# Sample rows of the input projection as fp32 products on four column strips, and one add ahead of the sums of squares

## The chip, the core and the metric

The kernel runs on one core of one Trainium2 chip. The metric is device time in microseconds, the median of repeated runs; the profile is of one further execution, and all rows below come from it. The engines are TensorE (PE, with its weight loads PEld), VectorE (DVE), ScalarE (ACT), GpSimd (POOL) and SyncE (SP, which issues most of the loads).

## What is computed

One step of a decoder layer with width 1024 on 2048 prompt rows and 32 sample rows (8 sequences of 4 tokens). Both sets of rows go through the same input projection, whose 3072 columns are six blocks of 512, and then through their own attention and retention:

```python
hp = rms_norm(xp, norm_mix_g[l], NORM_EPS)
dq, dk, dv, rq, rk, rv, rg = project_mixer_inputs(hp, w_in[l], *tab_p)
...
hs = rms_norm(xs, norm_mix_g[l], NORM_EPS)
sq, sk, sv, tq, tk, tv, tg = project_mixer_inputs(hs, w_in[l], *tab_s)
```

with

```python
y = xf * lax.rsqrt(jnp.mean(xf * xf, axis=-1, keepdims=True) + eps)
...
z = h @ w_in_l
dq, dk, dv, rq, rk, rv, rg = jnp.split(z, SPLIT_POINTS, axis=-1)
```

All tensors are fp32. The per-row factor of the norm is applied after the product, to its result; only the gain g is multiplied into the rows before it.

## The kernel before

The program is: projection, mixer (attention and retention, decode of the sample rows, output projection), and the two halves of the FFN. `projection` runs over four token groups g of 512 rows (four tiles of 128), and in each over the six blocks of 512 weight columns in the order 1, 2, 0, 3, 4, 5 (keys, values, queries, retention q and k, retention v, gate). "First block", "fourth block" and so on below count in that order.

Precision: every fp32 operand of a large product is split into a high part in the type fp32r and the rest (`split`, L121 to L124: a cast on ACT, a subtraction on DVE), and a product is three fp32r products, h.wh, l.wh and h.wl (`terms`, L292, lines L296 to L298). A block has 1024 rows of weights, loaded as four panels kp of two 128-row slices (512 KB each) into the tile `wr` of pool `early`, which has two buffers (`load_w`, L174; the load is L176 on SP), and split into `wh` and `wl` with six buffers each. A tile of tokens takes 24 products of 512 columns (8 slices k, 3 terms) into one bank of PSUM with the tag `z`, of which there are four. In the first block of a group the four tiles go side by side (k is the outer loop), so all four banks are in use; in the others one tile after the other.

The 32 sample rows are a fifth tile (t = NQ) in group 0 only. Their columns of x are loaded (`xsr`, L206), squared (`xsq`, L208), multiplied by the gain and split into `xs`, with the high and low halves side by side as 64 columns; `sample_terms` (L307 to L309) multiplies these 64 columns with `wh` and with `wl`, 16 products a block, into a fifth `z` bank. `fold` (L300) copies the first 32 partitions of the result and adds the second 32 (`add_halves`). This tile is the last of each block in group 0.

The factor of the norm: the squares of x are added up over the panels in `sq` [128, 2, 512] (L195, L197). `scales` (L217) multiplies each of its eight 128-column pieces with a column of ones (L221, eight plain fp32 products of one column, two accumulating per tile), the same for the sample rows (L226), copies the sums and takes the power -0.5 on POOL (`rsqrt_mean`). The results `rstd` and `rstd8` are what the first reader of `z` scales with: `krow` in `put_qk` (L318) on ACT for queries and keys.

Retention per prompt tile (`retention`, L379) runs in the fifth block and uses two banks with the tag `r`. The FFN has two products for the sample rows that are already in the form of plain fp32 on strips: L1207, tile `sz`, four strips of 32 rows, 256 columns, two rounds; and L1314, tile `sacc`, strips of 32 rows, 512 columns.

Most of the order on each engine is set by a scheduler when the kernel is built: it takes the program's order and the dependences and places each instruction by its own estimate of times, and each engine then runs its list strictly in that order. `keep_in_program_order` pins single instructions. A buffer of a tile tag goes to the next tile when the last reader is done.

## Time and profile before

| | |
|---|---|
| time, median of 3 runs | 2707.18 us (2699.53 to 2709.26) |
| profiled execution, its own time | 2718.03 us |
| its span | 2716.3 us |
| mean granted clock of PE | 0.984 of full speed |
| busy PE / DVE / ACT / POOL | 2617.5 / 1526.0 / 1064.9 / 1009.1 us |
| chain that ended last: PE / DVE / DMA / ACT | 85% / 4% / 4% / 3% |
| projection, fp32r products of the prompt rows (L296 to L298) | 768 of each of three lines, about 303 us a line |
| projection, products of the sample rows (L308, L309) | 48 of each line |

How to read it: a plain fp32 product of the program shows as two records in the trace, an fp32r product as one. A record's duration contains the filling of the array, so the time that a product holds PE is read from start to start of neighbours: 0.23 us for 512 columns at full clock, where each record is 0.39 us long. The stages lie at 0 to about 680 us (projection), to 1360 (mixer), to 2270 (first half of the FFN) and to the end. In the timelines the number in front is the start from the span's begin, the second the length; a bracket gives the idle time of the engine before the row and what ended it. An SP row is the issue of a transfer, not its length.

### The profile page before, as it was taken

The numbers are of one execution on the slowest core, as the hardware profiler recorded it, in microseconds if no ns is written. First come the engines' busy times: TensorE is split into PE (matmuls) and PEld (weight loads), VectorE is DVE, ScalarE is ACT, GpSimd is POOL, SyncE is SP. The second block draws the span as 40 slices with busy tenths as digits, with TensorE's granted clock in tenths as the row PEclk, the third lists the DMA queues.
The fourth block names the chain that finished last, engine by engine and source line by source line (L and its number), as shares of the span: only waits on it lengthen the run. The fifth ranks groups of instructions, "written<-read, shape, count | busy, mean of one in ns | idle before, by whom it ended". The sixth has DMA issues, their size and how long they took to land.

```text
span 2716.3 us, 35504 instructions
## 1 busy us (share of the span) xinstructions
PE 2617.5 (96%) x13180; PEld 2097.4 (77%) x13180; DVE 1526.0 (56%) x2296; ACT 1064.9 (39%) x2051; POOL 1009.1 (37%) x1032
## 2 busy tenths in 40 slices
PE   8999999999888999997989999999999999999998
PEld 6777788787666888886768778786777777788886
DVE  5554544543667677675365555585665665345364
ACT  4343343432556555554243233352332333333342
POOL 1000000011662133324456556557877884003111
PEclk9999999999899999999999999999999999999999
DMA  7436545364995464624442222354434436744463
GB/s 240 129 105 186 155 146 152 113 182 128 257 254 132 129 170 126 156 81 155 133 182 83 96 101 86 105 174 171 148 131 167 149 130 216 257 143 148 141 208 120
DMA packets 166347, 413.35 MB, mean 152 GB/s; under 512 B 19376, under 2 KB 54896, under 8 KB 164384
## 3 DMA queue, kind: packets, MB, share of 16 engines
q1 hardware_dynamic: 100176, 259.63, 29.3%
q0 software_dynamic: 56784, 147.27, 18.6%
q10 hardware_dynamic: 9216, 4.20, 0.6%
q8 instruction: 104, 1.70, 0.3%
q14 instruction: 67, 0.55, 0.1%
HBM read 287.95 MB, written 123.08 MB: 151 GB/s over the span
## 4 chain that ended last, share of the span: by engine, by line
PE 85%; DVE 4%; DMA 4%; ACT 3%; issue 3%; POOL 2%; ACTq 0%; SPq 0%; POOLq 0%; DVEq 0%
PE fps L1162 27%; PE ops L1378 15%; PE z L298 7%; PE z L297 7%; PE z L296 7%; PE op L854 4%; PE sp L796 2%; PE sp L799 2%; PE atp L843 2%; PE cz L956 2%; PE cz L955 2%; PE cz L957 1%; ACT p L814 1%; DMA w<-w_ffn_out 1%; PE op L399 1%
## 5 line engine op out<-in xcount | busy, mean ns | idle before, releaser
L1162 PE MATMUL fps<-xh,wh 128*128 128x512 f32 x1232 | 485.2, 396 | 4.5 <-ACT xh L123 4.5
L1162 PE MATMUL fps<-xh,wl 128*128 128x512 f32 x1232 | 482.2, 391 | 0.0
L1162 PE MATMUL fps<-xl,wh 128*128 128x512 f32 x1232 | 481.4, 391 | 0.0
L296 PE MATMUL z<-wh,xh 128*128 128x512 f32 x768 | 302.9, 396 | 8.5 <-ACT xh L190 8.5
L298 PE MATMUL z<-wl,xh 128*128 128x512 f32 x768 | 303.6, 396 | 0.0
L297 PE MATMUL z<-wh,xl 128*128 128x512 f32 x768 | 302.6, 394 | 0.0
L1162 PEld LDWEIGHTS fps<-xh,wh 128*128 128x128 f32 x1232 | 232.2, 189 | 71.1 <-issue 11.6
L1162 PEld LDWEIGHTS fps<-xh,wl 128*128 128x128 f32 x1232 | 232.0, 188 | 58.3 <-issue 9.2
L1162 PEld LDWEIGHTS fps<-xl,wh 128*128 128x128 f32 x1232 | 232.2, 188 | 47.1
L124 DVE TENSOR_TENSOR xl<-xl,xh 128x1024 fp32r<-128x1024 f32 (+1 forms) x133 | 149.3, 1145 | 203.7 <-ACT xh L123 203.7
L1378 PE MATMUL ops<-vh,xh 128*128 128x512 f32 x616 | 239.6, 392 | 6.8 <-ACT u L1406 4.7
L1378 PE MATMUL ops<-vh,xl 128*128 128x512 f32 x616 | 239.7, 391 | 0.0
L1378 PE MATMUL ops<-vl,xh 128*128 128x512 f32 x616 | 238.3, 391 | 0.0
L124 DVE TENSOR_TENSOR wl<-w,wh 128x512 fp32r<-128x512 f32 x132 | 150.4, 1150 | 119.0 <-ACT wh L123 118.9
L800 DVE TENSOR_REDUCE mx<-sp 128x1 f32<-128x1024 f32 (+4 forms) x192 | 168.7, 908 | 83.9 <-PE sp L799 66.1
L124 DVE TENSOR_TENSOR wl<-wt,wh 128x512 fp32r<-128x512 f32 x176 | 194.7, 1111 | 30.4 <-ACT wh L123 30.4
L123 ACT CAST xh<-xl 128x1024 fp32r<-128x1024 f32 (+1 forms) x133 | 111.6, 868 | 221.5 <-DMA xl<-hop_d 200.2
L123 ACT CAST wh<-wt 128x512 fp32r<-128x512 f32 x176 | 109.1, 621 | 193.2 <-PE fps L1162 163.6
L124 DVE TENSOR_TENSOR wl<-wr,wh 128x1024 fp32r<-128x1024 f32 x96 | 117.2, 1222 | 109.4 <-ACT wh L123 107.7
L296 PEld LDWEIGHTS z<-wh,xh 128*128 128x128 f32 x768 | 144.7, 189 | 38.7 <-ACT xh L190 8.5
L123 ACT CAST wh<-w 128x512 fp32r<-128x512 f32 x132 | 81.8, 620 | 229.3 <-PE fps L1162 185.7
L298 PEld LDWEIGHTS z<-wl,xh 128*128 128x128 f32 x768 | 144.8, 188 | 31.7 <-issue 0.7
(308 smaller groups left out, 5008.7 us busy)
## 6 DMA issues: line engine op xcount, KB each, us to landing
wr<-w_in SPq DMA_DIRECT2D x96, 512.0 KB
w<-w_ffn_in SPq DMA_DIRECT2D x44, 1024.0 KB
xl<-hop_d SPq DMA_DIRECT2D x77, 512.0 KB
hop_d<-so POOLq DMA_DIRECT2D x88, 256.0 KB
kst<-k_d POOLq DMA_DIRECT2D x36, 512.0 KB
hop_d<-h POOLq DMA_DIRECT2D x66, 256.0 KB
qd<-q_d POOLq DMA_DIRECT2D x64, 256.0 KB
xop_d<-xt POOLq DMA_DIRECT2D x56, 256.0 KB
```

Of the source, the lines that this page charges most:

```text
L123: nc.scalar.copy(hi, src)
L124: nc.vector.tensor_tensor(lo, src, hi.bitcast(F32), ALU.subtract)
L296: mm(z, h[:, j, c], wh[:, j], start=k == 0, stop=False)
L297: mm(z, l[:, j, c], wh[:, j], start=False, stop=False)
L298: mm(z, h[:, j, c], wl[:, j], start=False, stop=k == KT - 1)
L796: nc.tensor.matmul(sp[:, o : o + nn], q[:, 2 * mp, sl], k, start=True, stop=False)
L799: nc.tensor.matmul(sp[:, o : o + nn], q[:, 2 * mp + 1, sl], k, start=False, stop=True)
L800: nc.vector.tensor_reduce(mx[:, c : c + 1], sp[:, :w], AX.X, ALU.max, negate=True)
L843: nc.tensor.transpose(tp[:, j, :], pt[b // 8][0][:, P * (b % 8) : P * (b % 8) + P], self.ident)
L854: self.nc.tensor.matmul(st["o"], ats[(b - lo) // 4][:, (b - lo) % 4, :], vs[b // 4][:, b % 4, :], start=b == 0, stop=b == st["i"],)
L1162: i = nc.tensor.matmul(bank, w[:, c], v, start=first and k == 0 and n == 0, stop=k == half - 1 and n == 2, skip_group_check=True,)
L1378: nc.tensor.matmul(bank, x[:, c], w, start=first and n == 0, stop=end and n == 2, skip_group_check=True)
```

## The change

- The sample rows of a block are now eight plain fp32 products of the unsplit rows (`xsr`, gain multiplied in, 32 columns) with the unsplit weight panels (`samples`). Slice k = 4 half + q goes to strip q, that is to partitions 32 q to 32 q + 31 of one bank; each strip adds up two slices. The bank has the tag `r` instead of `z`. `samples(b)` is called at the head of a block instead of in the place of the fifth tile; in each half the strips are written 3, 2, 1, 0, and 2, 1 and 0 are pinned in that order.
- `fold` adds up four strips instead of two halves: one copy and three adds.
- `xs` and its split are gone.
- In group 0 the panels kp 2 and 3 have buffers of their own (`wr2`, two), so that four raw panels are there at once. In the other groups all four panels use the two buffers `wr` as before. In group 0 a panel's buffer is now also held until the sample products have read it.
- In `scales` the two halves of `sq` are added on DVE first; four products of one column take the place of eight.

```diff
--- before.py
+++ after.py
@@ -171,8 +171,17 @@
                 self.rope_t = {4 * g + i: rp[:, i] for i in range(4)}
                 self.rope_t[NQ] = rope_s
 
+                raws = {}
+                if g == 0:
+                    sa = tc.tile_pool(reuse_waits="tile", name="sa", bufs=1)
+                    sap = sa.__enter__()
+
                 def load_w(b, kp):
-                    wr = early.tile([P, 2, 512], F32, tag="wr", name="wr", bufs=2)
+                    if g == 0 and kp > 1:
+                        wr = sap.tile([P, 2, 512], F32, tag="wr2", name="wr2", bufs=2)
+                    else:
+                        wr = early.tile([P, 2, 512], F32, tag="wr", name="wr", bufs=2)
+                    raws[b, kp] = wr
                     nc.sync.dma_start(wr, a["w_in"][b, :, 2 * kp : 2 * kp + 2, :])
                     wh = pw.tile([P, 2, 512], F32R, tag="wh", name="wh", bufs=6)
                     wl = pw.tile([P, 2, 512], F32R, tag="wl", name="wl", bufs=6)
@@ -200,15 +209,28 @@
                     if kp == 0:
                         nc.gpsimd.dma_start(rp, a["rope"][:, 4 * g : 4 * g + 4])
                 if g == 0:
-                    sa = tc.tile_pool(reuse_waits="tile", name="sa", bufs=1)
-                    sap = sa.__enter__()
                     xsr = sap.tile([P, KT, NS], F32, name="xsr")
                     nc.sync.dma_start(xsr, a["xt"][:, :, S:])
                     xsq = sap.tile([P, KT, NS], F32, name="xsq")
                     nc.scalar.activation(xsq, xsr, AF.Square)
-                    xs = sap.tile([P, KT, 2, NS], F32R, name="xs")
                     nc.vector.tensor_tensor(xsr, xsr, bc(gmix, 2, [P, KT, NS]), ALU.mult)
-                    self.split(xs[:, :, 0], xs[:, :, 1], xsr)
+
+                def samples(b):
+                    z = ps.tile([P, 512], F32, tag="r", name="zsm", bufs=2)
+                    for half in range(2):
+                        for q in (3, 2, 1, 0):
+                            k = 4 * half + q
+                            i = nc.tensor.matmul(
+                                z[NS * q : NS * q + NS],
+                                xsr[:, k, :],
+                                raws[b, k // 2][:, k % 2],
+                                start=half == 0,
+                                stop=half == 1,
+                            )
+                            if q < 3:
+                                keep(i)
+                    return z
+
                 ss = rows.tile([P, 8], F32, tag="ss", name="ss", bufs=2)
                 rstd = rows.tile([P, 8], F32, tag="rstd", name="rstd", bufs=2)
                 rstd8 = rows.tile([P, 8], F32, tag="rstd8", name="rstd8", bufs=2)
@@ -216,11 +238,9 @@
 
                 def scales():
                     sp = ps.tile([P, 8], F32, tag="tp", name="ssp", bufs=2)
+                    nc.vector.tensor_tensor(sq[:, 0], sq[:, 0], sq[:, 1], ALU.add)
                     for i in range(4):
-                        for j in range(2):
-                            nc.tensor.matmul(
-                                sp[:, i : i + 1], sq[:, j, P * i : P * i + P], ones, start=j == 0, stop=j == 1
-                            )
+                        nc.tensor.matmul(sp[:, i : i + 1], sq[:, 0, P * i : P * i + P], ones, start=True, stop=True)
                     if g == 0:
                         for k in range(KT):
                             nc.tensor.matmul(sp[:NS, 4:5], xsq[:, k], ones, start=k == 0, stop=k == KT - 1)
@@ -239,6 +259,8 @@
                     if bi:
                         for kp in range(KT // 2):
                             load_w(b, kp)
+                    if g == 0:
+                        zsm = samples(b)
                     first = []
                     if bi == 0:
                         first = [ps.tile([P, 512], F32, tag="z", name="z", bufs=4) for _ in range(4)]
@@ -251,17 +273,12 @@
                         m = NS if t == NQ else P
                         if i < len(first):
                             z = first[i]
+                        elif t == NQ:
+                            z = self.fold(rows, zsm, 512)
                         else:
                             z = ps.tile([P, 512], F32, tag="z", name="z", bufs=4)
                             for k in range(KT):
-                                if t < NQ:
-                                    self.terms(z, xh, xl, wts, b, k, i)
-                                    continue
-                                wh, wl = wts[b, k // 2]
-                                both = xs[:, k].rearrange("p c q -> p (c q)")
-                                self.sample_terms(z, both, wh[:, k % 2], wl[:, k % 2], k == 0, k == KT - 1)
-                        if t == NQ:
-                            z = self.fold(rows, z, 512)
+                                self.terms(z, xh, xl, wts, b, k, i)
                         r1 = rstd[:m, i : i + 1]
                         r8 = rstd8[:m, i : i + 1]
                         if b in (0, 1):
@@ -301,7 +318,8 @@
         nc = self.nc
         zs = pool.tile([NS, n], F32, tag="zs", name="zs", bufs=1)
         nc.vector.tensor_copy(zs, z[:NS, :n])
-        self.add_halves(zs, z, 1)
+        for q in range(1, 4):
+            nc.vector.tensor_tensor(zs, z[NS * q : NS * q + NS, :n], zs, ALU.add)
         return zs
 
     def sample_terms(self, z, both, wh, wl, first, last):
```

The scheduler moves instructions as well. Three places follow, each of the list before and of the list now; the lists are those of the program, without times, and a number behind a name tells buffers apart.

PE at the end of token group 0. Before, the last sample product (`xs` with the last `wl`) and the first products of group 1 behind it:

```order
L309 MATMUL z_1610<-wl_1447,xs_318 64x512
L296 MATMUL z_1701<-wh_1644,xh_1636 128x512 [waits Activation_49]
L297 MATMUL z_1701<-wh_1644,xl_1637 128x512
L298 MATMUL z_1701<-wl_1645,xh_1636 128x512
L296 MATMUL z_1702<-wh_1644,xh_1636 128x512 [waits Activation_49]
L297 MATMUL z_1702<-wh_1644,xl_1637 128x512
L298 MATMUL z_1702<-wl_1645,xh_1636 128x512
```

Now: the last retention tile's `up`, the sixth group of sample products (`zsm`, reading the raw panels `wr` and `wr2`), and the first product of group 1:

```order
L428 MATMUL up_1373<-rv_1343,kd_1371 64x128 [waits DVE_49]
L428 MATMUL up_1373<-rv_1343,kd_1371 64x128 x3
L223 MATMUL zsm_1414<-wr_1396,xsr_314 32x512 [waits DMAHW2_49,DVE_49]
L223 MATMUL zsm_1414<-wr_1396,xsr_314 32x512
L223 MATMUL zsm_1414<-wr_1390,xsr_314 32x512 [waits DMAHW1_49]
L223 MATMUL zsm_1414<-wr_1390,xsr_314 32x512
L223 MATMUL zsm_1414<-wr2_1408,xsr_314 32x512 [waits DMAHW4_49]
L223 MATMUL zsm_1414<-wr2_1408,xsr_314 32x512
L223 MATMUL zsm_1414<-wr2_1402,xsr_314 32x512 [waits DMAHW3_49]
L223 MATMUL zsm_1414<-wr2_1402,xsr_314 32x512
L313 MATMUL z_1659<-wh_1602,xh_1594 128x512 [waits Activation_49]
```

The first product of group 1 waited for ACT's `xh` and `wh` in both. The sample products of the sixth block stand behind all 576 prompt products of group 0, and the first of them waits for DVE to have read the `r` bank of the last retention tile. Those of the other five blocks stand in one piece at the head of their block (in the first after 47 products), except that in the fourth four transposes stand between the first four and the last four.

SP at the same place. Before: the four weight loads of group 1's first block, with an `xr` load between them, and the stores `cat_d` of the gated retention rows of group 0 behind them:

```order
L176 DMA wr_1642<-w_in 128x1024 [waits DMAHW3_49,DVE_49]
L176 DMA wr_1658<-w_in 128x1024 [waits DMAHW4_49,DVE_49]
L185 DMA xr_1666<-xt 128x2x512 [waits Activation_49]
L176 DMA wr_1674<-w_in 128x1024 [waits DMAHW5_49,DVE_49]
L176 DMA wr_1690<-w_in 128x1024 [waits DMAHW6_49,DVE_49]
L377 DMA cat_d_72<-ro_1204 128x512 [waits DVE_49]
L377 DMA cat_d_72<-ro_1270 128x512 [waits DVE_49]
L377 DMA cat_d_72<-ro_1336 128x512 [waits DVE_49]
L185 DMA xr_1682<-xt 128x2x512 [waits DVE_49]
```

Now: the four loads of the sixth block of group 0, the stores, and then the first two loads of group 1, `wr_1600` and `wr_1616`:

```order
L185 DMA wr_1390<-w_in 128x1024 [waits DMAHW1_49,DMAHW6_49,DVE_49,PE_49]
L185 DMA wr_1396<-w_in 128x1024 [waits DMAHW5_49,PE_49]
L185 DMA wr2_1402<-w_in 128x1024 [waits DMAHW0_49,DVE_49,PE_49]
L185 DMA wr2_1408<-w_in 128x1024 [waits DMAHW7_49,PE_49]
L395 DMA cat_d_72<-ro_1183 128x512 [waits DVE_49]
L395 DMA cat_d_72<-ro_1249 128x512 [waits DVE_49]
L395 DMA cat_d_72<-ro_1315 128x512 [waits DVE_49]
L185 DMA wr_1600<-w_in 128x1024 [waits DMAHW2_49,PE_49,Activation_49]
L185 DMA wr_1616<-w_in 128x1024 [waits DMAHW1_49,PE_49]
```

The loads of group 1's first block moved from ahead of the stores to behind them, and wait for PE now, where they waited for DVE.

PE at the sums of squares of group 1. Before, `z_1701` to `z_1704` are the four tiles of the first block; the sums stand in the middle of their products, 61 behind the start of the block:

```order
L296 MATMUL z_1704<-wh_1676,xh_1668 128x512
L297 MATMUL z_1704<-wh_1676,xl_1669 128x512
L298 MATMUL z_1704<-wl_1677,xh_1668 128x512
L296 MATMUL z_1701<-wh_1676,xh_1668 128x512
L221 MATMUL ssp_1753<-ones_237,sq_1633 128x1 [waits DVE_49]
L221 MATMUL ssp_1753<-ones_237,sq_1633 128x1 x7
L297 MATMUL z_1701<-wh_1676,xl_1669 128x512
L298 MATMUL z_1701<-wl_1677,xh_1668 128x512
L296 MATMUL z_1702<-wh_1676,xh_1668 128x512
```

Now the four tiles are `z_1659` to `z_1662`, and `z_2017` is the first tile of the second block:

```order
L313 MATMUL z_1662<-wh_1650,xh_1642 128x512
L314 MATMUL z_1662<-wh_1650,xl_1643 128x512
L315 MATMUL z_1662<-wl_1651,xh_1642 128x512
L243 MATMUL ssp_1711<-ones_237,sq_1591 128x1 [waits DVE_49]
L243 MATMUL ssp_1711<-ones_237,sq_1591 128x1 x3
L313 MATMUL z_2017<-wh_1995,xh_1594 128x512 [waits Activation_49]
L314 MATMUL z_2017<-wh_1995,xl_1595 128x512
L315 MATMUL z_2017<-wl_1996,xh_1594 128x512
L313 MATMUL z_2017<-wh_1995,xh_1594 128x512
```

The sums moved behind all 96 products of the first block. In groups 2 and 3 they stand after 69 and 64 products (58 and 58 before), in group 0 after 84 (82).

In the mixer's first part, where the decode of the sample rows is woven into the attention, the lists hold the same instructions in another order. Behind that they agree.

## Rows read from the trace of the kernel before

**Rows 1.** The page, part 1: busy us (share) and instructions by engine

```profile
PE 2617.5 (96%) x13180; PEld 2097.4 (77%) x13180; DVE 1526.0 (56%) x2296; ACT 1064.9 (39%) x2051; POOL 1009.1 (37%) x1032
```

**Rows 2.** Waits of PE, 8 to 680 us: total us, times, longest

```profile
PE z L296 <- ACT xh L190: 8.5, 1, 8.5
PE sop L475 <- DMA sr<-state_ret: 0.7, 1, 0.7
```

**Rows 3.** Windows: us, busy of PE, PEld, DVE, ACT, POOL, PEclk, DMA share, GB/s

```profile
191.00:680.00 489.00, 488.18 (x2399) 392.12 (x2397) 231.69 (x480) 173.94 (x308) 50.12 (x67) 1.00 0.53 154
680.00:900.00 220.00, 189.72 (x1309) 140.51 (x1310) 140.13 (x284) 124.18 (x322) 102.72 (x128) 0.92 0.76 204
```

**Rows 4.** Timeline of PE, 33 to 43 us: start, us, instruction, [idle before]

```profile
35.09 0.40 PE L308 MATMUL z<-wh,xs 128*64 128x512 f32 x1
38.77 0.40 PE L296 MATMUL z<-wh,xh 128*128 128x512 f32 x1
```

**Rows 5.** Timeline of PE around one strip group of the FFN's input, 1420 us

```profile
1420.92 0.39 PE L1162 MATMUL fps<-xh,wl 128*128 128x512 f32 x1
1421.24 1.07 PE L1207 MATMUL sz<-w,xs 128*32 128x256 f32 x16
1422.24 0.50 PE L1162 MATMUL fps<-xh,wh 128*128 128x512 f32 x1
1422.58 0.40 PE L1162 MATMUL fps<-xl,wh 128*128 128x512 f32 x1
```

**Rows 6.** Timeline of PE around two strip groups of the FFN's second product

```profile
1883.74 1.93 PE L1314 MATMUL sacc<-w,hs 128*32 128x512 f32 x6 [2.74 <-DMA w<-w_ffn_out]
1885.60 0.80 PE L1162 MATMUL fps<-xh,wh 128*128 128x512 f32 x1
...
1925.85 1.06 PE L1314 MATMUL sacc<-w,hs 128*32 128x512 f32 x6
1926.84 0.50 PE L1162 MATMUL fps<-xh,wh 128*128 128x512 f32 x1
```

**Rows 7.** Timeline of PE around the sums of squares of group 0

```profile
29.42 1.84 PE L221 MATMUL ssp<-ones,sq 128*128 128x1 f32 x16
31.19 0.67 PE L226 MATMUL ssp<-ones,xsq 128*32 128x1 f32 x16
31.79 0.50 PE L297 MATMUL z<-wh,xl 128*128 128x512 f32 x1
```

**Rows 8.** Groups of DVE by form: busy us, mean ns, idle us before

```profile
L141 DVE TENSOR_TENSOR rot<-rot,rtmp 128x512 f32<-128x512 f32 x16 | 11.0, 688 | 0.2
```

**Rows 9.** Timeline of SP, issues of weight loads

```profile
190.46 0.33 SPq L176 DMA_DIRECT2D wr<-w_in  x1
194.65 0.38 SPq L176 DMA_DIRECT2D wr<-w_in  x1
```

**Rows 10.** Timeline of ACT, the casts that waited for those loads, and krow

```profile
33.63 1.27 ACT L318 ACTIVATE krow<-z,rstd 128x512 f32<-128x512 f32 x2 [6.38 <-POOL rstd L119]
...
194.09 1.05 ACT L123 CAST wh<-wr 128x1024 fp32r<-128x1024 f32 x1 [1.49 <-DMA wr<-w_in]
201.21 1.05 ACT L123 CAST wh<-wr 128x1024 fp32r<-128x1024 f32 x1 [4.31 <-DMA wr<-w_in]
```

**Rows 11.** Timeline of PE around two idle stretches

```profile
890.01 0.50 PE L796 MATMUL sp<-kst,qd 128*128 128x512 f32 x1 [2.56 <-ACT p L814]
...
1838.83 1.44 PE L1314 MATMUL sacc<-w,hs 128*32 128x512 f32 x6 [2.82 <-DMA w<-w_ffn_out]
1840.19 0.80 PE L1162 MATMUL fps<-xh,wh 128*128 128x512 f32 x1
1842.87 0.40 PE L1162 MATMUL fps<-xh,wh 128*128 128x512 f32 x1
```

**Rows 12.** Windows of the stretch 50 to 70 us, columns as above

```profile
50.00:60.00 10.00, 10.00 (x48) 8.05 (x47) 1.32 (x4) 2.23 (x4) 2.56 (x4) 1.00 1.03 263
60.00:70.00 10.00, 10.00 (x45) 7.35 (x45) 3.63 (x4) 3.35 (x4) 0.00 (x0) 1.00 0.88 268
```

## Prediction

> **What bounds the kernel now.** I read the page's busy shares first, then PE's waits, then the table by stage, then the timelines of PE, SP and ACT where the change acts. PE is busy for 96% of the span, DVE for 56% [rows 1]. In the projection that is tighter still: from 8 to 680 us PE waits twice, once for its first operand at the start and once for 0.7 us [rows 2], and from 191 to 680 us it is busy for 488.2 of 489 us at full clock [rows 3]. So in this stage time on PE is time, and anything added to DVE or ACT is free until PE has to wait for it. In the mixer's first 220 us the opposite holds: PE stands idle for 30.3 us and the clock is at 0.92 [rows 3]; the decode rows are woven in there.
>
> **Part 1, the sample products.** One block's 16 products last from 35.09 to 38.77 us, 3.68 us, right up to the next product [rows 4]; six blocks are 22.1 us. What takes their place has a model in the FFN: plain fp32 products of 32 columns on strips. Three strips of 512 columns (six records, two a product) hold PE 0.99 us at full clock and 1.86 us at half [rows 6]. The difference, 0.87 us, is what one round over the strips streams at full clock, however many strips take part. Eight products of 256 columns, two rounds on four strips, go from 1421.24 to 1422.24 us [rows 5]: 1.00 us for two half rounds, so the fourth strip is free too. The group also starts 0.09 us late against the 0.23 us step of its neighbours, and the product behind it takes 0.34 us instead of 0.23: 0.33 us of edges in all beyond the 0.87. A block of the new kind has two full rounds, 2 x 0.87 + 0.33 = 2.07 us, six 12.4, and 0.3 more because the group of the fourth block is cut by four transposes in the order. Gain: 22.1 - 12.7 = **9.4 us**. [...]
>
> **Part 2, the sums of squares.** Eight products of one column take 1.77 us, from 29.42 to 31.19 [rows 7]. Four go in each of four token groups: 4 x 0.88 = **3.5 us** gained. The new DVE add per group and the two more adds per fold are 4 + 12 adds of 512 columns, 0.69 us each [rows 8], 11 us on an engine that is busy less than half of the stage [rows 3]; the xs split that goes was as well hidden. In group 0 the add stands in DVE's queue behind the first fold, and 37 products (8 us) stand on PE between the two things it joins; without that cover its 0.7 us would be seen once.
>
> **Part 3, the entry of group 1.** This is new and on the path. A raw panel now stays in its buffer until the sample products have read it. In blocks 1 to 5 the next loads have a whole block, over 21 us, to come. But the last group waits for a "r" bank behind the last retention tile, so it stands after all 576 products of token group 0, and the two "wr" buffers that group 1 wants are free only then. Before, these panels were loaded and split long ahead. The chain: the first round ends 1.06 us after its start [rows 6], the load takes 3.63 us from issue to the cast at the same place of the old program (190.46 to 194.09, [rows 9, 10]), the cast 1.05 us [rows 10]: the first product starts 5.74 us after the group, which itself holds PE for about 1.86. **Idle 3.9 us.** The other row, a load with more transfers around it, took 6.56 us (194.65 to 201.21, [rows 9, 10]), which would make it 6.8; I take the first because, as there, nothing but small tables and state follows on SP. The clock goes with it: after 2.82 us idle the strip group took 1.36 instead of 0.99 us, and six products from 1840.19 to 1842.87 took 2.68 instead of 1.36 us [rows 11], **1.7 us** together. What is queued behind the two loads on SP (bias tables, state, the third xr) has 11 us of products before anyone needs it.
>
> **Part 4, the sums in group 1.** The order puts them after all 96 products of the first block, where they stood after 61. All four "z" banks then hold finished tiles that krow can't drain without rstd, so the next product waits for the chain of copy, power on POOL and first krow. In group 0 PE went on at 31.79 us and the first of the two krow, half of 1.27 us from 33.63, ended at about 34.3 [rows 7, 10]: **2.5 us**, then under cover, now bare. I add no clock loss: a wait of 2.56 us left products at 0.50 us, one of 2.82 us did not [rows 11]. The ends are nothing, if the bank comes free sooner, and 2.5 + 1.7 us.
>
> **Part 5, the mixer.** Its first 220 us are woven anew in the static order, with the same work. I take nothing; as bounds I take 8 us either way, about a quarter of PE's idle time there [rows 3].
>
> **Sum.** -9.4 - 3.5 + 3.9 + 1.7 + 2.5 = **-4.8 us**. The profiled execution, 2718.03 us with a span of 2716.3, would become 2713.2. It stands 10.9 us above the median of the runs, so the forecast is 2707.18 - 4.8 = **2702.4 us**, -0.18%. A measurement of this kernel can tell about 0.5%, 13.5 us, from no change, so this is "same".
>
> **Rivals.**
> A. The two new waits don't appear, because the buffers or the banks are free earlier than I read: -12.9 us, 2694.3, at the very edge of 0.5%. For: PE did not wait anywhere here before [rows 2]. Against: the order names a PE wait on the load and one on the product.
> B. Slower. The panels of the fourth block can be asked for only after the third block's sample products, at about 62 us, when the stores of k and v fill the engines (share 1.03 and 0.88, [rows 12]). The fourth block's sample products stand at its head, 96 products and eight transposes or 22.7 us later, and need all four panels. If the loads, one behind the other, get a quarter of the 263 GB/s, each 512 KB take 8 us and the last lands after 32: 9.3 us late, with the clock 11.0, and the run takes 2713.4 us. It decides from 5.7 us a load on; at 8 it turns the gain into a loss of 6 us. For: the 6.56 us of [rows 9, 10], which would give 2707.6. Against: the four loads alone would be carried in 8 us at that rate, and what they share it with is some 4 MB.
> C. The mixer's new weave costs or gives 8 us: 2710.4 or 2694.4.
> D. The strips don't overlap as in the FFN: eight products one after another, 8 x 0.87 + 0.33 = 7.3 us a block against 3.68, so +21.7 us in place of the gain of 9.4, and 2733.5 in all. [rows 5, 6] speak against it.
>
> [...]
>
> **How the numbers follow.** Forecast 0.55, A 0.18, B 0.10, C 0.06 each way, D 0.02, E 0.03. Faster than 2693.6: half of A with some help of the mixer, half of C's good side and a rest of the forecast, 0.16. Slower than 2720.7: D, and B or C together with a longer load in part 3, 0.07. Same: 0.77. The range runs from A with a little help of the mixer, 2690, to C's bad side with the 6.56 us load in part 3 (+2.9), 2714.
>
> **What would show it.** Right: six groups of 16 zsm records of about 1.9 us each; 8 ssp records a group; an idle stretch of PE near 182 us of 3 to 5 us put down to ACT's cast behind a wr load, with products of 0.6 us behind it; a second one of some 2.5 us about 30 us later behind ssp, put down to krow. Wrong: zsm groups of over 2.5 us, waits of PE for wr before zsm in blocks 1 to 4, no gap at group 1's start, or a first stretch of the mixer that is more than 8 us off.

## The result and the profile after

The changed kernel takes 2715.17 us (median of 11 runs, 2706.45 to 2724.68) against 2707.18 us of the kernel before on the same chip: a ratio of 1.0028, 95% interval 1.0015 to 1.0041. Forecast were 2702.4 us and a range of 2690 to 2714. The change costs some 8 us where 4.8 us of gain were forecast; under the 0.5% that the prediction calls "same", but the interval excludes zero, and two more comparisons say the same (1.0036 and 1.0035, below). The chips differ by more than that (before has medians of 2707 us on this one and of 2714.5 to 2717 us on others), so whole kernels are compared by their ratio to before on the same chip.

The profiled execution took 2706.45 us (span 2704.7), that of before 2718.03. This pair alone would say the opposite of the runs, and so would the second pair below (2713.44 and 2720.66 us). The first pair differs by the mixer (below), so stages have to be compared one by one. The page's part 1, which answers to [rows 1]:

```profile
PE 2602.1 (96%) x13148; PEld 2082.4 (77%) x13148; DVE 1523.5 (56%) x2311; ACT 1067.0 (39%) x2050; POOL 1012.7 (37%) x1032
```

The waits of PE from 8 to 680 us (total, times, longest), which answer to [rows 2]:

```profile
PE z L313 <- ACT krow L336: 8.5, 2, 7.0
PE z L313 <- ACT xh L199: 8.5, 1, 8.5
PE z L313 <- ACT wh L123: 4.1, 1, 4.1
PE tp L344 <- DVE krow L371: 0.5, 1, 0.5
```

Beside the start (8.5 us, as before) there are three new waits of over 1 us, one for a weight cast (4.1 us) and two for krow (7.0 and 1.5 us), and one of 0.5 us at a transpose. The windows answer to [rows 3]; three short ones show the granted clock behind the two long waits and between them:

```profile
191.00:680.00 489.00, 481.40 (x2338) 386.62 (x2336) 234.82 (x473) 176.31 (x306) 48.64 (x66) 0.99 0.53 157
680.00:900.00 220.00, 196.06 (x1405) 147.62 (x1405) 148.01 (x304) 130.67 (x342) 104.97 (x129) 0.96 0.78 211
188.00:193.00 5.00, 4.75 (x14) 3.76 (x15) 4.73 (x6) 3.06 (x4) 0.00 (x0) 0.66 0.83 260
193.00:212.00 19.00, 19.00 (x87) 15.72 (x85) 14.29 (x19) 11.52 (x14) 0.00 (x0) 1.00 0.72 245
219.70:224.00 4.30, 4.22 (x11) 3.37 (x12) 2.76 (x9) 1.54 (x3) 0.00 (x0) 0.55 0.72 249
```

The timeline of PE at the places that the prediction speaks of (start, us, instruction, idle before and its releaser):

```profile
20.67 0.39 PE L314 MATMUL z<-wh,xl 128*128 128x512 f32 x1
20.99 1.92 PE L223 MATMUL zsm<-wr,xsr 128*32 128x512 f32 x16
22.84 0.50 PE L315 MATMUL z<-wl,xh 128*128 128x512 f32 x1
...
31.41 0.95 PE L243 MATMUL ssp<-ones,sq 128*128 128x1 f32 x8
32.29 0.67 PE L246 MATMUL ssp<-ones,xsq 128*32 128x1 f32 x16
...
39.20 0.50 PE L313 MATMUL z<-wh,xh 128*128 128x512 f32 x1 [1.45 <-ACT krow L336]
...
182.26 1.92 PE L223 MATMUL zsm<-wr,xsr 128*32 128x512 f32 x16
188.25 0.50 PE L313 MATMUL z<-wh,xh 128*128 128x512 f32 x1 [4.07 <-ACT wh L123]
...
211.79 0.95 PE L243 MATMUL ssp<-ones,sq 128*128 128x1 f32 x8
219.78 0.79 PE L313 MATMUL z<-wh,xh 128*128 128x512 f32 x1 [7.04 <-ACT krow L336]
...
223.68 0.39 PE L313 MATMUL z<-wh,xh 128*128 128x512 f32 x1
```

The strip groups last 1.85 us (20.99 to 22.84) and the four sums 0.88 us, as priced. The wait at the entry of group 1 is there, 4.07 us. The wait at the sums of group 1 is not 2.5 but 7.04 us, and nine products behind it take 3.90 us instead of 2.1. A third wait, 1.45 us in group 0, was not foreseen.

Summing, over all rows of PE's timeline up to the end of the projection (679.9 us before, 685.7 after), the time from a row to the next one without the idle part (what a record lasts beyond that shows in the sums of the sample rows before, where products of one column start 0.04 us apart and each record lasts 0.17 us):

| us of PE in the projection | before | after |
|---|---|---|
| sample products | 22.4 | 11.4 |
| sums of squares, token rows | 6.9 | 3.5 |
| products of the token rows | 541.2 | 546.5 |
| everything else | 100.2 | 102.0 |
| idle | 9.2 | 22.3 |
| end | 679.9 | 685.7 |

14.4 us come back from samples and sums; 13.1 us go to new idle time (12.6 of them in the three waits), 5.3 us to the token products (slow clock behind the waits, and the edges of the strip groups, which this sum books on the product behind a group) and 1.8 us to the rest.

**Where the 7.04 us come from.** DVE, ACT, POOL and SP in that stretch of the changed kernel:

```profile
208.13 1.22 DVE L124 TENSOR_TENSOR wl<-wr,wh 128x1024 fp32r<-128x1024 f32 x1
210.03 1.23 DVE L124 TENSOR_TENSOR wl<-wr,wh 128x1024 fp32r<-128x1024 f32 x1 [0.68 <-ACT wh L123]
215.23 1.23 DVE L124 TENSOR_TENSOR wl<-wr,wh 128x1024 fp32r<-128x1024 f32 x1 [3.98 <-ACT wh L123]
216.49 0.16 DVE L249 COPY ss<-ssp 128x4 f32<-128x4 f32 x1
216.92 1.23 DVE L124 TENSOR_TENSOR wl<-wr,wh 128x1024 fp32r<-128x1024 f32 x1
```

```profile
214.15 1.04 ACT L123 CAST wh<-wr 128x1024 fp32r<-128x1024 f32 x1 [4.16 <-DMA wr<-w_in]
...
219.04 1.26 ACT L336 ACTIVATE krow<-z,rstd 128x512 f32<-128x512 f32 x2 [2.16 <-POOL rstd L119]
```

```profile
216.93 2.08 POOL L119 TENSOR_TENSOR rstd<-rstd,half 128x4 f32<-128x4 f32 x1 [32.01 <-DVE rstd L118]
```

```profile
209.38 9.12 SPq L185 DMA_DIRECT2D wr<-w_in  x4
```

The sums are done at 212.7 us. Their copy out of PSUM takes 0.16 us but stands on DVE behind the split of a panel of the next block. That split waits for ACT's cast, which waits for a load that SP could issue only at 209.38, when a raw buffer came free. So the copy runs at 216.49, 3.7 us late, and the power on POOL takes 2.08 us where the same power takes 1.01 in the kernel before. Group 0 is the same in small: its sums end at 33.0 us, three splits and an add of the fold stand ahead of the copy, which runs at 36.8, and krow comes 1.45 us too late.

The queue isn't new in group 1. The kernel before shows it at the same place:

```profile
204.75 1.84 PE L221 MATMUL ssp<-ones,sq 128*128 128x1 f32 x16
```

```profile
208.59 1.23 DVE L124 TENSOR_TENSOR wl<-wr,wh 128x1024 fp32r<-128x1024 f32 x1 [1.81 <-ACT wh L123]
209.85 0.16 DVE L229 COPY ss<-ssp 128x4 f32<-128x4 f32 x1
```

There the sums end at 206.59 us and the copy runs 3.3 us later, behind a split that had waited for its cast. In both programs DVE's list has all four splits of the second block ahead of this copy. Before, PE had 35 products of the first block left and waited for nothing. In group 0 of the kernel before, where the prediction read its price, DVE was waiting for the sums:

```profile
31.89 0.15 DVE L228 COPY ss<-ssp 32x1 f32<-32x1 f32 x1 [3.81 <-PE ssp L226]
```

### The profile page after: what moved, and what is told of

Its sections match the earlier page's. It is cut to its first block, busy times and chain, and to the rows that moved or that the text cites. A ratio compares the mean times of both kernels' runs of the same rounds, so it can differ in the third digit from the quotient of the medians.

```text
span 2704.7 us, 35461 instructions
## 1 busy us (share of the span) xinstructions
PE 2602.1 (96%) x13148; PEld 2082.4 (77%) x13148; DVE 1523.5 (56%) x2311; ACT 1067.0 (39%) x2050; POOL 1012.7 (37%) x1032
## 4 chain that ended last, share of the span: by engine, by line
PE 83%; DMA 5%; issue 4%; DVE 4%; ACT 2%; POOL 2%; POOLq 0%; ACTq 0%; SPq 0%; DVEq 0%
PE fps L1180 28%; PE ops L1396 15%; PE z L315 6%; PE z L313 6%; PE z L314 6%; PE op L872 3%; PE sp L814 2%; PE sp L817 2%; PE atp L861 2%; PE cz L973 2%; PE cz L974 2%; PE cz L975 2%; DMA cat<-cat_d 1%; DMA pg<-kcache,idx 1%; PE op L422 1%
## 5 line engine op out<-in xcount | busy, mean ns | idle before, releaser
L124 DVE TENSOR_TENSOR wl<-w,wh 128x512 fp32r<-128x512 f32 x132 | 143.8, 1100 | 121.2 <-ACT wh L123 121.0
L124 DVE TENSOR_TENSOR wl<-wt,wh 128x512 fp32r<-128x512 f32 x176 | 188.3, 1075 | 32.9 <-ACT wh L123 32.9
```

Source lines behind the costliest of these rows:

```text
L124: nc.vector.tensor_tensor(lo, src, hi.bitcast(F32), ALU.subtract)
```

## The experiments

**The sample products of the last block in a z bank.** They then need no bank behind the last retention tile, and the fold follows at once:

```diff
 def samples(b):
-    z = ps.tile([P, 512], F32, tag="r", name="zsm", bufs=2)
+    if b == order[-1]:
+        z = ps.tile([P, 512], F32, tag="z", name="zsm", bufs=4)
+    else:
+        z = ps.tile([P, 512], F32, tag="r", name="zsm", bufs=2)
...
     zsm = samples(b)
+    if b == order[-1]:
+        zsm = self.fold(rows, zsm, 512)
...
-    z = self.fold(rows, zsm, 512)
+    z = zsm if b == order[-1] else self.fold(rows, zsm, 512)
```

> The sample products of the last block of token group 0 get a bank of the four-deep z ring and are folded at once, so they stand at the head of that block and free their weight panels 96 products earlier; everything else is as in the changed kernel. Theory W (the 8 us are PE's waits in the projection, all from weight panels that come free late): the 4.07 us wait at the entry of group 1 goes with its 1.6 us of slow clock, and since the loads of group 1 are early again the sums stand after 69 products and not 96, so the 7.04 us wait and its 1.9 us go too: 14.6 us less, about 2700.6 us. Rival Q (the wait at the sums comes from the order on DVE and ACT alone, whatever the loads): only 5.7 us less, 2709.5 us, with a wait of 5 to 7 us behind ssp still there. Rival M (the 8 us come from the new weave of the mixer): at most 3 us less, 2712 us or more.

Measured: ratio to before 0.9967 (0.9954 to 0.9979), -9 us, some 16 us under the changed kernel, of which the projection alone shows 15 (below; this version also has the mixer's order of before). In its profile PE waits from 8 to 668 us for nothing but the start, and the sums of group 1 pass under cover:

```profile
PE z L318 <- ACT xh L199: 8.5, 1, 8.5
```

```profile
198.24 0.95 PE L246 MATMUL ssp<-ones,sq 128*128 128x1 f32 x8
199.05 0.48 PE L318 MATMUL z<-wh,xh 128*128 128x512 f32 x1
```

```profile
199.23 0.16 DVE L252 COPY ss<-ssp 128x4 f32<-128x4 f32 x1 [2.42 <-PE ssp L246]
```

DVE now waits for the sums and not the other way round. Theory W holds: both waits of group 1 have one root, the panels held until the last sample products.

**The queue alone.** With the loads as late as in the changed kernel:

```diff
 for kp in range(KT // 2):
-    load_w(b, kp)
+    if bi == 1 and g in (1,):
+        with tc.issue_after(scale.ins):
+            load_w(b, kp)
+    else:
+        load_w(b, kp)
```

(scale is the instruction of line 118 on the sums; what load_w puts on DVE then stands behind it.)

> The changed kernel, but in group 1 the second block's weight splits on DVE are queued behind the scale of the sums; PE's order is the same, and ACT's first two krow now stand ahead of three of the casts. The loads are as late as before. If the queue on DVE and ACT is what made the wait 7.04 instead of 2.5 us: ssp ends at 212.74 us, copy and scale 0.4, the power on POOL 2.08, the first krow 0.7, so the wait is 3.2 to 3.5 us; with the clock's 1.9 us unchanged the kernel takes 3.6 us less than the changed one, about 2711.6 us. If POOL or the loads of weights set the end: the wait stays at 6 us or more, 2714 to 2716 us.

Measured: 1.0011 (0.9999 to 1.0023), 4 to 5 us under the changed kernel, a difference that the two intervals don't settle; the mixer's order on PE is a third one here, too. The projection alone (below) says 3 to 4 us. In the profile the wait is now 3.17 us:

```profile
211.98 0.16 DVE L249 COPY ss<-ssp 128x4 f32<-128x4 f32 x1 [4.56 <-PE ssp L243]
```

```profile
215.11 0.79 PE L318 MATMUL z<-wh,xh 128*128 128x512 f32 x1 [3.17 <-ACT krow L341]
```

So the order on DVE and ACT made 7.04 out of 3.2 us. The rest of it, 3.2 us, is the chain of copy, power and krow itself, which the prediction had at 2.5; the power takes 1.91 us here.

**The sums by themselves**, in either direction: put back to eight products in the changed kernel, and made four products in the kernel before.

```diff
+nc.vector.tensor_tensor(sq[:, 0], sq[:, 0], sq[:, 1], ALU.add)
 for i in range(4):
-    for j in range(2):
-        nc.tensor.matmul(sp[:, i : i + 1], sq[:, j, P * i : P * i + P], ones, start=j == 0, stop=j == 1)
+    nc.tensor.matmul(sp[:, i : i + 1], sq[:, 0, P * i : P * i + P], ones, start=True, stop=True)
```

> The changed kernel with the eight products of the sums as before (no add on DVE). By part 2 of the prediction 3.5 us more on PE. The sums of group 1 then stand after 87 products instead of 96, 2 us of cover, so by theory W the wait there is about 5 us: the sum is 1.5 us more than the changed kernel, 2716.7 us. If the add on DVE is itself what made the sums late, the wait falls below 3 us and the time to 2713 us or less.

> The kernel before with the change of the sums alone (one add on DVE, four products), its sample products as they were. By part 2: 3.5 us less, 2703.7 us; the sums of group 1 stand after 73 products there, so no wait of PE in the projection. If the add makes a wait by itself, PE idles behind ssp or krow in group 0 or 1 and the gain is gone: 2707 us or more.

Measured: 1.0049 (1.0034 to 1.0064) and 1.0016 (1.0001 to 1.0032). The first is 4 to 6 us over the changed kernel instead of 1.5. In its profile the wait at the sums of group 1 is 3.60 us, not 5, and the last token product of the projection starts at 680.77 us, 2 to 4 us later than in the three profiles of the changed kernel (679.00, 677.09, 676.82). So the four sums with their add save time in the projection; the rest of the difference is behind it, where this kernel has another order, too. The second is a miss of sign: 4 us slower than before instead of 3.5 faster, though its projection ends 2.2 us earlier in the profile. New there is one wait of PE, for krow in group 0:

```profile
35.96 0.45 PE L306 MATMUL z<-wh,xs 128*64 128x512 f32 x1 [0.94 <-ACT krow L316]
```

The loss must lie behind the projection. That asked for a cleaner yardstick.

**The projection alone.** Mixer and FFN are left out (two lines of the program's run), the order in the projection stays.

> The kernel before with the mixer and the FFN left out: the projection alone, with the same order on PE, DVE and ACT, so that the other stages' own spread is out of the time. The yardstick for the next three. In the profile of the whole kernel the projection ends at 679.9 us, so this takes 690 to 700 us with the last stores; its runs should lie within 3 us of each other if the spread of the whole kernel (2699.5 to 2713.3 us) comes from the mixer and the FFN.

> The changed kernel with the mixer and the FFN left out. Theory W (the waits for late panels outweigh the gain on PE inside the projection): 5 to 6 us over the projection before (profile of the whole kernels: 685.7 against 679.9 us). Rival M (the projection is no slower, the loss is the mixer's new weave): within 1 us or faster.

> The version with the last block's sample products in a z bank, mixer and FFN left out: by theory W 11 to 12 us under the projection before and 17 us under the changed one (12.7 us of gain on PE, no new wait). Rival M: about the same as the changed one.

> The kernel before with only the change of the sums, mixer and FFN left out. The whole kernel with that change was 0.16% slower than before, though its projection ended 2.2 us earlier in its profile. If the rest of that loss is the mixer's weave: 2 to 3.5 us under the projection before (3.4 us of products less, up to 1 us of wait for krow in group 0). If the projection itself is slower: over it.

> The changed projection alone, with the second block's splits and casts of group 1 behind the scale of the sums. In the whole kernel's profile this cut the wait behind ssp from 7.04 to 3.17 us; the changed projection's own profile has 5.53 us there. If the queue is all of the difference: 2.4 to 3.9 us under the changed projection's 694.95 us, so 691 to 692.6 us. If only the profile's run differed: within 1 us of 694.95.

| projection alone, us | median (runs) | to before |
|---|---|---|
| before | 690.74 (689.54 to 691.27) | |
| changed | 694.95 (693.12 to 697.13) | +4.2 |
| z bank | 679.80 (679.34 to 680.90) | -10.9 |
| before with the four sums | 688.11 (687.89 to 688.65) | -2.6 |
| changed, splits behind the scale (another chip) | 690.98 (689.88 to 692.08) | +0.2 |

The runs lie within some 2 us of each other (4 in the changed one), so most of the whole kernel's spread of 14 us is behind the projection. The new waits outweigh the gain on PE inside the projection; rival M fails for that half. The splits behind the scale take the changed projection from 694.95 us (693.98 in a second series, below) to 690.98, which is what the wait lost in the profile (7.04 to 3.17 us). But 4.2 us are half of what the whole kernel loses, and the four sums lose 4 us in the whole kernel while their projection gains 2.6. Something behind it costs both of them 4 to 7 us.

**Both kernels once more**, for second profiles, and the z bank version with the splits of group 0 behind the scale too:

> The kernel before against itself: ratio 1.000 within 0.0013. What is asked is the second profile. If the length of the mixer's first 220 us is set by the order of its instructions, PE stands idle for 28 to 33 us in the 220 us behind the projection, as in the first profile (30.4 us), and the mixer lasts 688 to 692 us again. If it goes by the run, the idle time may as well be 23 us, as in the changed kernel's profile, or 34.

> The changed kernel again, on another chip. Theory W plus weave (4.2 us from the projection alone, the rest from the mixer): ratio 1.0015 to 1.0041 as before, and the projection's three waits at their places (4.07, 7.04 and up to 1.45 us in the first profile). If nothing but the projection counts: 1.0015 (4.2 us). The first profile was of the fastest of 11 runs, with 23 us of idle PE in the mixer's first 220 us; if that goes by the run, this profile has 25 to 34 us and a mixer of 685 to 697 us instead of 677.

> The z bank version with one thing more: in group 0 the second block's weight splits on DVE stand behind the scale of the sums, so that the first krow no longer hangs on the arrival of two panels. In the z bank version's profile PE did not wait there, in the changed kernel's it waited 1.45 us. By theory W 0 to 1.5 us less than the z bank version, ratio to before 0.996 to 0.997; if the order of the mixer's start is worth more than that, anything up to 3 us off either way.

Measured: before against itself 0.9998 (0.9982 to 1.0015); the changed kernel 1.0036 (1.0018 to 1.0054); the third 0.9964 (0.9947 to 0.9980). This last beats both kernels by 0.36% and more, but isn't told apart from the z bank version. From the mixer's first wait for p to the first FFN product that waits for its input, the changed kernel's mixer lasted 673.8 us in its first profile and 688.2 in this one, before's 687.9 and 690.6: the length goes by the run, and no profile shows the loss.

**The mixer's order.** Both kernels run the same work in the mixer, in another static order. Six memsets on a free tile ahead of group 3 shift the scheduler's reckoning so that the changed kernel gets the mixer's order of before (its last 8732 instructions on PE stand as in before; the changed kernel shares 8321 with before; mixer and FFN have some 9050):

```diff
 n = len(tiles)
+if g == 3:
+    junk = rows.tile([P, 512], F32, tag="zs", name="junk", bufs=1)
+    for _ in range(6):
+        nc.vector.memset(junk, 0.0)
```

They change the projection as well: in group 1 one split now stands behind the copy of the sums, the copy comes at once, and the wait at the sums is 3.73 us (3.6 in the second profile), with no wait for krow in group 0:

```profile
212.28 0.16 DVE L253 COPY ss<-ssp 128x4 f32<-128x4 f32 x1 [0.25 <-PE ssp L247]
```

```profile
215.97 0.79 PE L317 MATMUL z<-wh,xh 128*128 128x512 f32 x1 [3.73 <-ACT krow L340]
```

So this version needs its own projection alone.

> The changed kernel with six idle memsets on DVE ahead of group 3, which change nothing but the scheduler's reckoning: the projection keeps its order on PE up to the start of group 1 and its three waits, and the last 8732 products of the program stand as in the kernel before, not as in the changed one (which shares the last 8321 with it; the mixer and FFN are some 9050). If the new weave of the mixer costs the half of the loss that the projection alone doesn't show: ratio to before 1.0015 (4.2 us), some 4 us under the changed kernel. If the weave is worth nothing and the rest came by the projection in the whole program: ratio 1.003, as the changed kernel.

> The same kernel as weave_old_1, for a narrower interval, since 4 us are asked for where one comparison gives 3.5 either way: ratio 1.0015 if the weave costs 4 us, 1.003 if it costs nothing.

> The changed kernel beside weave_old on the same chip: ratio 1.003 again, the mean of 1.0028 and 1.0036, if these two were not chance; 1.0015 if only the projection's 4.2 us are real.

> The projection alone of the version with the mixer's order of before. By its profile's waits (4.1 and 3.7 us, none in group 0) it is 2 to 3 us under the changed projection's 694.95 us: 692 to 693 us. Then some 7 us of the 10 between it and the changed kernel are the mixer's order. If it takes 688 us or less, the projection explains most of it and the mixer's weave little.

> The changed projection alone on the same chip as proj_weave_old: 694 to 696 us again.

> The projection of before alone on that chip: 690 to 691.5 us again, 4 to 5 us under the changed one.

| | whole kernel, ratio to before | projection alone, us |
|---|---|---|
| changed, mixer's order of before | 0.9994 (0.9979 to 1.0009) and 1.0002 (0.9991 to 1.0013) | 693.15 (691.69 to 693.58) |
| changed | 1.0035 (1.0020 to 1.0049) | 693.98 (692.50 to 695.13) |
| before | 1 | 691.38 (690.29 to 692.19) |

On one chip the changed kernel takes 2727.06 us, with the other order 2715.75 and 2717.72: 10 us less, of which the projection explains 0.8. The whole kernels' profiles agree: the last token product starts at 676.45 and 676.28 us with the memsets, 0.4 to 2.7 us ahead of the changed kernel (674.08 and 674.74 in the kernel before). So the order behind the projection is worth some 9 us between these two; that is twice what was expected of it. The lists of ACT, DVE and SP differ there in places as well; most of all, the decode's gathers stand elsewhere on POOL. The order on POOL at some of these gathers (pg) and the loads of q (qd), in the changed kernel:

```
L727 DMA qd<-q_d_63 64x1024 x2
L554 DMA pg<-kcache,idx 128x512 x4
L727 DMA qd<-q_d_60 64x1024 x2
L554 DMA pg<-vcache,idx 128x512 x8
L727 DMA qd<-q_d_61 64x1024 x2
```

and with the memsets, as in the kernel before:

```
L558 DMA pg<-kcache,idx 128x512 x4
L731 DMA qd<-q_d_63 64x1024 x2
L731 DMA qd<-q_d_60 64x1024 x2
L558 DMA pg<-vcache,idx 128x512 x4
L731 DMA qd<-q_d_61 64x1024 x2
L558 DMA pg<-vcache,idx 128x512 x4
```

The two kernels above with a third order on PE (the splits behind the scale, and the eight sums) have the changed kernel's order of transfers on POOL, and both lose behind the projection: 3 us by difference of the medians (+3.0 whole, +0.2 alone) and some 7 us (+13.3 whole, about 6 in the profile). The z bank version and the memsets have the order of before on both engines and lose 2 us and nothing. This points at the gathers, but they weren't moved by themselves, and the profiles can't show it. From the wait at the mixer's start to the first FFN product that waits for its input they have 688.3 us for the changed kernel and 688.5 for the other:

```profile
686.27 0.58 PE L814 MATMUL sp<-kst,qd 128*128 128x256 f32 x1 [2.08 <-ACT p L832]
1374.58 0.80 PE L1180 MATMUL fps<-xh,wh 128*128 128x512 f32 x1 [3.98 <-ACT xh L123]
```

```profile
685.91 0.38 PE L818 MATMUL sp<-kst,qd 128*128 128x256 f32 x1 [2.79 <-ACT p L836]
1374.40 1.22 PE L1184 MATMUL fps<-xh,wh 128*128 128x512 f32 x2 [4.35 <-ACT xh L123]
```

## Why the prediction was wrong, by its own steps

The three comparisons make 7.6, 9.8 and 9.5 us of loss, 9 in the mean, against -4.8: a miss of 14 us. About 8 of it lie in the projection (+3.4 in the mean of 4.2 and 2.6, against -4.8), nearly 6 behind it.

**Part 1, right.** -9.4 forecast. The sample products fell from 22.4 to 11.4 us; the edges, by the z bank version, whose projection alone has a granted clock of 0.994 to 0.996 (0.985 to 0.987 in the changed one alone), are 1.8 us (its token products take 543.0 against 541.2 us): -9.2. Rival D falls by the same row: 1.85 us a group. So does E, less than full gain from four strips, which had a chance of 0.03: no run shows a loss with four column strips of 512 columns.

**Part 2, right on PE, wrong on DVE.** 3.4 us gained of 3.5. "The new DVE add per group and the two more adds per fold" were called hidden on an engine "busy less than half of the stage". In group 0 the copy of the sums came 3.8 us behind their end, with splits and a fold ahead of it, and PE waited 1.45 us (0.41 in the second profile, nothing over 0.4 in the third; it hangs on when two panels land). The four sums alone show it too: PE waits 0.94 us there, and 3.4 - 0.9 is the 2.6 us that their projection gains.

**Part 3, right.** 3.9 us idle and 1.7 us of clock forecast; 4.07 us, and 12 products in 4.34 us where 2.8 are usual, so 1.5 us. The granted clock is 0.66 from 188 to 193 us, behind 4.07 us without work, and 1.00 from 193 to 212 us. Rival B didn't come: no wait of PE at the fourth block's panels.

**Part 4, the step that failed.** The place and the releaser were right, the size was not: 2.5 us and no clock loss against 7.04 us idle and 1.8 us at the slow clock (granted 0.55). No clock loss was read from the wait of 2.56 us [rows 11], whose row is the first product alone; the four products from 890.01 to 891.52 us take 1.51 us where 0.92 are usual, at a granted clock of 0.65. In the three profiles the wait is 7.04, 6.49 and 5.69 us. The 2.5 us were read in group 0 of the old program [rows 7, 10], where DVE was waiting when the sums came. In group 1 the second block's splits stand ahead of the copy. They stood there before, too, and the copy was 3.3 us late then, under cover: read there, from the end of the sums at 206.59 us to the second scaling of rstd at 211.33 and with a krow of 0.7, the chain is 5.4 us. The late loads of part 3 made these splits later still. The prediction asked who waits for the held panels, and left out that their splits stand in the same queue as the copy. Of the 6.3 us by which the term was too small, 3.9 are that queue (with it taken away 3.17 us were left), 1.8 the clock, and the rest, 0.6 us, goes with POOL's longer power. Wait and clock together, 8.9 us, are more than twice the upper bound of 4.2.

**Part 5, inside its bounds, but half of the surprise.** Nothing was taken, with 8 us either way. By difference the new weave costs the changed kernel some 5 to 6 us against before, and 9 us against the same kernel with the old order; the two figures differ by about as much as their intervals. The prediction had no row that gave a direction. What in the new order costs the time stays open. It is hardly chance: the four-sums kernel, woven anew too, loses 7 us behind the projection (+4.3 against -2.6), while the z bank version, which keeps before's last 8732 products, loses 2 (-9.0 against -10.9), within its interval of 3 us.

**The numbers.** The range ended at 2714, 1.2 us under the median. The upper end already put two unhappy ends together, the mixer's 8 us and the longer load of part 3; none of its cases had part 4 beyond its bound, and the runs had that and most of the mixer's bound at once. Each alone would have stayed inside the range.

## To carry to other kernels

A short instruction that frees a buffer or a bank is as late as what stands ahead of it in its engine's queue: here a copy of 0.16 us ran 3.7 us late, behind a split that waited for its panel. Price such a chain at the place where it will stand, with what is queued there, also where the old trace hides it under cover, and not by a place where the engine was idle; and when a change holds a buffer longer, follow the loads behind it into every queue that uses their data. Where a scheduler orders the whole program, take an early stage out by itself to measure it, and expect the stages behind it to move with no edit of theirs: here by some 9 us, between two orders of the same mixer.

## What was not expected of the hardware

**One profile isn't the kernel.** The profiled execution of the changed kernel was 9.3, 10.0 and 10.8 us under the median of the other runs of its series (2706.45 to 2715.7, 2713.44 to 2723.5, 2716.34 to 2727.2). The z bank version with the splits of group 0 behind the scale had it 10.5 under, before's first 10.9 over (2718.03 to 2707.18) and its second 2.9 over, the two with the old mixer order 0.7 and 2.8 under. In the projection alone it was within 2.4 us. The profiled execution was the first of its series each time, so profiling and being first can't be told apart. So a loss of 9 us in the mixer left no row to read. One number of the other runs goes with it, PE's mean granted clock: on one chip 0.985 in the kernel before, 0.981 in the changed one and 0.983 with the old order. The changed kernel's profiled execution there had 0.985, its other eight 0.979 to 0.983. That the lower clock makes the loss isn't shown; it may follow from PE's idle time.

**A power on POOL beside a split on DVE.** The 128x4 power on the sums of group 1 took 1.01 us in the kernel before and in the z bank version. In the changed kernel it took 2.08 us where a split of 1.23 us had started on DVE 0.01 us ahead of it, and 1.91 us in the run with the splits behind the scale, where two splits ran from 212.26 us beside it:

```profile
212.43 1.91 POOL L119 TENSOR_TENSOR rstd<-rstd,half 128x4 f32<-128x4 f32 x1 [28.25 <-DVE rstd L118]
```

In the changed kernel's second profile the split began 0.39 us behind the power, which took 1.01 us. Both long powers end 0.86 us behind the end of the split that had started ahead of them (218.15 to 219.01, 213.48 to 214.34). A third in the changed kernel, 1.32 us from 535.39 us, ends 0.88 us behind an add of DVE that had started 0.24 us ahead. A fourth is not like these: in the kernel before a power took 2.85 us from 191.79 us and ended 0.87 us behind a split that had started only at 192.56, with two copies on DVE between them. What holds the power up isn't shown: no run moved a split for this alone.
